# Reading the moving operand of 512-column products as two halves in turn

## The chip, the core and the metric

The kernel runs on one core of one Trainium2 chip. The metric is device time in microseconds (us) of one execution; the times given are medians over runs. In the profile, PE is TensorE (the matrix engine), PEld its loading of the stationary operand, DVE is VectorE, ACT is ScalarE, POOL is GpSimd and SP the engine from whose queue most transfers are issued. A TensorE product takes a stationary operand of 128 x 128, which is loaded first, and streams a moving operand of up to 512 columns past it; the result is added into a PSUM bank of 512 float columns per partition, of which there are eight.

## The reference

One layer of an encoder on 512 tokens with 1024 features. The mixer has two branches, bidirectional retention and a spatial gating unit (SGU), both fed by one input projection of 7168 columns; then comes a gated feed-forward part with a convolution of width 3:

```python
h = _rmsnorm(x, g_pre_mix)
q, k, v, g, u, sv, a_ret, a_sgu = jnp.split(h @ w_in, ...)
y_ret = _retention_branch(q, k, v, g, ret_decay_logit, w_ret_o)
y_sgu = _sgu_branch(u, sv, sgu_ln_g, sgu_ln_b, w_spatial, b_spatial, w_sgu_o)
merged = jax.nn.sigmoid(a_ret) * y_ret + jax.nn.sigmoid(a_sgu) * y_sgu
x = x + _rmsnorm(merged @ w_out, g_post_mix)
h2 = _rmsnorm(x, g_pre_ffn)
x = x + _rmsnorm(_conv_gated_mlp(h2, w_up, conv_w, conv_b, w_down), g_post_ffn)
```

All inputs and the output are float32. Nearly all the work is in the products with w_in, w_ret_o, w_sgu_o, w_out, w_up and w_down.

## The kernel before

Every float32 product is made of three faster ones. A helper `split` (L100) writes a value's high part (float32 rounded to the type fp32r, by ScalarE) and its low part (the difference, by VectorE); `mm3` (L230) then issues high x high, high x low and low x high into the same bank. So each product of the algorithm is three TensorE instructions, at L231, L232 and L233, or at L543 to L545, L924 to L926 and so on where they are written out. The weights come in from HBM through SP's queue as blocks of 128 x 1024 (`w_block`, `w_form`, `w_down`, fetched some blocks ahead by `w_get`), and are split on ScalarE and VectorE at L95 and L102 before TensorE can use them.

The stages, in order, all on one core:

- q and k (L336 to L351): eight banks, each 128 output features x 512 tokens; stationary is the weight, moving is `xh`/`xl`, the scaled input with features on partitions and 512 tokens along the row. The first k step (L342) runs in parts, as its operands arrive. Eight evacuations follow (L428 to L433).
- v, sv and g (`t_group`, L533): here tokens are stationary and the weight is moving, 512 columns of it; between the parts come the retention products of 256 columns.
- u and the gates (`Pair`, L746): a scheme with seven products in place of eight, on operands of 256 columns: `forms` (sums and differences) and halves T0, T1 of `xh`/`xl` taken by `Pair.x` (L768).
- w_ret_o and w_sgu_o (`f_block`, L735, called by `gated_pair`): weight stationary, 512 tokens moving (`ogh`, `yh` and their low parts). L886 and L893 multiply their results by the gates, from PSUM.
- w_out (`Down`, L906): tokens stationary, 512 columns of the weight moving. After each tile of 128 tokens come the norms, and `turn` (L985) transposes the tile on TensorE and writes `h2h` (L994, ScalarE) and `h2l` (L997, VectorE), features on partitions, 128 tokens at a time.
- w_up: `early` (L1017) makes the first four blocks in two halves of 256 tokens while the last tiles of w_out are still finished; then blocks of 512 tokens by `f_block`, and from block 4 to 19 couples, in which a `Pair` on `h2h`/`h2l` and their forms is mixed with two calls of `f_block` (48 products of 512 columns and 84 of 256 in a couple). `tile_done` makes the convolution and the gate from the banks.
- w_down (`products`, `add_whole`): products of 256 columns, then the last norm.

What sets the order: the instructions of each engine run in the order in which they were scheduled when the program was built, and each waits on semaphores for its operands. The tiles are aligned by hand: `slot` (L142) and the pads of `hi192`/`lo64` place weights at 0, 64 or 192 bytes against the row of the moving operand.

On the host, `_pairs` and `_rows` arrange the weights into blocks; the arrangement is not part of the device time.

## Time and profile before

| | us |
|---|---|
| time, median of 3 runs (818.19 to 819.24) | 818.48 |
| span of the profiled execution | 817.4 |
| TensorE, a product in flight | 809.1 |
| VectorE busy | 659.9 |
| ScalarE busy | 441.3 |
| GpSimd busy | 86.0 |

The page has no time of the profiled execution other than its span, from its first instruction to its last. A group's line gives the source line, engine, operation, output and inputs, the shape (stationary rows * columns, then moving and output size), the count, the busy time and the mean length of one. For a TensorE product that length runs from its entry into the array until its modelled end, so that lengths of neighbours overlap. A line of the timeline gives start, length and instruction. A line of a stretch gives the stretch, its length, then busy time and count for PE, PEld, DVE, ACT and POOL, then the granted TensorE clock, the share of the DMA engines and their rate.

### The profile page before, as it was taken

To read this page: it belongs to the slowest core of one execution; us is meant where nothing else is said; L and a number is where in the kernel's file an instruction comes from. 1 tells how busy PE (TensorE), PEld (TensorE's weight loads), DVE (VectorE), ACT (ScalarE), POOL (GpSimd) and SP (SyncE) were. 2 spreads that over 40 slices of the span, in tenths; PEclk is the share of its full clock that TensorE was granted. 3 is DMA by queue.
4 is the path that set the end of the run, shared out by engine and by line. 5 is a ranking of instruction groups with operands and counts; after the bars stand their busy time and mean duration, and the time that the engine had idled before them with its cause. 6 is when DMAs were issued, how large, how long until landed. Compare 5 with 4: busy or idle time off the path is not lost. (4 is left out here: it accounts for less than half of the span.)

```text
span 817.4 us, 13292 instructions
## 1 busy us (share of the span) xinstructions
PE 809.1 (99%) x5163; PEld 730.4 (89%) x5163; DVE 659.9 (81%) x1115; ACT 441.3 (54%) x777; POOL 86.0 (11%) x93
## 2 busy tenths in 40 slices
PE   9999999999999999999999999999999999999996
PEld 7888888888999999999988898899999898999996
DVE  7479897877898777767765659989999989987877
ACT  6546445536675444444445577556666666544441
POOL 0010000110001111132210210110111200000001
PEclk9999999999999999999999999999999999999998
DMA  8733222221333332233349111333333341233244
GB/s 287 259 117 103 78 79 77 77 79 65 103 103 105 104 103 90 91 103 103 107 165 335 53 51 66 104 103 104 104 103 103 103 156 52 77 130 110 97 155 155
DMA packets 29647, 93.24 MB, mean 114 GB/s; under 512 B 3536, under 2 KB 4432, under 8 KB 29584
## 3 DMA queue, kind: packets, MB, share of 16 engines
q1 hardware_dynamic: 27360, 86.76, 31.5%
q0 software_dynamic: 1360, 4.46, 1.6%
q10 hardware_dynamic: 864, 1.18, 0.4%
q8 instruction: 40, 0.66, 0.3%
q14 instruction: 23, 0.19, 0.1%
HBM read 88.19 MB, written 4.19 MB: 113 GB/s over the span
## 5 line engine op out<-in xcount | busy, mean ns | idle before, releaser
L102 DVE TENSOR_TENSOR wl<-raw,wh 128x1024 fp32r<-128x1024 f32 (+1 forms) x92 | 108.5, 1187 | 42.5 <-PE ps L762 20.0
L95 ACT ACTIVATE wf<-raw 128x512 fp32r<-128x512 f32 x140 | 85.0, 626 | 99.3 <-PE ps L232 34.0
L102 DVE TENSOR_TENSOR wf<-raw,wf 128x512 fp32r<-128x512 f32 x140 | 106.5, 773 | 25.3 <-ACT wf L95 24.5
L762 PE MATMUL ps<-sh,wf 128*128 128x256 f32 x640 | 118.8, 277 | 0.2 <-ACT c L95 0.2
L95 ACT ACTIVATE wh<-raw 128x1024 fp32r<-128x1024 f32 (+2 forms) x96 | 93.3, 983 | 39.2 <-PE ps L545 15.8
L762 PEld LDWEIGHTS ps<-sh,wf 128*128 128x128 f32 x640 | 100.9, 188 | 1.0 <-ACT c L95 0.4
L232 PE MATMUL ps<-h2l,wh 128*128 128x512 f32 (+1 forms) x256 | 92.5, 363 | 0.0
L231 PE MATMUL ps<-h2h,wh 128*128 128x512 f32 (+1 forms) x256 | 92.4, 364 | 0.0
L233 PE MATMUL ps<-h2h,wl 128*128 128x512 f32 (+1 forms) x256 | 92.3, 361 | 0.0
L762 PE MATMUL ps<-sl,wf 128*128 128x256 f32 x320 | 88.5, 277 | 0.0
L543 PE MATMUL ps<-wh,xh 128*128 128x512 f32 x192 | 75.0, 391 | 0.0
L544 PE MATMUL ps<-wl,xh 128*128 128x512 f32 x192 | 74.8, 390 | 0.0
L545 PE MATMUL ps<-wh,xl 128*128 128x512 f32 x192 | 74.7, 389 | 0.0
L762 PEld LDWEIGHTS ps<-sl,wf 128*128 128x128 f32 x320 | 60.1, 188 | 0.6
L1170 PE MATMUL ps<-dl,fh 128*128 128x256 f32 x216 | 59.8, 277 | 0.0
L1170 PE MATMUL ps<-dh,fh 128*128 128x256 f32 x216 | 59.7, 277 | 0.0
L1170 PE MATMUL ps<-dh,fl 128*128 128x256 f32 x216 | 59.7, 277 | 0.0
L233 PEld LDWEIGHTS ps<-h2h,wl 128*128 128x128 f32 x256 | 48.0, 188 | 7.7
L231 PEld LDWEIGHTS ps<-h2h,wh 128*128 128x128 f32 x256 | 47.8, 188 | 7.2 <-ACT h2h L994 0.3
L232 PEld LDWEIGHTS ps<-h2l,wh 128*128 128x128 f32 x256 | 48.1, 188 | 6.6
L762 PE MATMUL ps<-xh,wf 128*128 128x256 f32 x288 | 53.9, 278 | 0.0
L95 ACT ACTIVATE dh<-raw 128x768 fp32r<-128x768 f32 (+1 forms) x36 | 33.6, 949 | 34.4 <-DVE raw L204 18.9
(314 smaller groups left out, 2037.4 us busy)
## 6 DMA issues: line engine op xcount, KB each, us to landing
raw<-wall SPq DMA_DIRECT2D x144, 512.0 KB, 3.6
x<-x SPq DMA_DIRECT2D x24, 256.0 KB, 6.2
x<-x POOLq DMA_DIRECT2D x8, 256.0 KB, 2.4
xT<-xT SPq DMA_DIRECT2D x7, 256.0 KB, 4.7
xT<-xT POOLq DMA_DIRECT2D x4, 256.0 KB, 3.3
out<-zg SPq DMA_DIRECT2D x4, 256.0 KB, 2.0
raw<-wall SPq DMA_DIRECT2D x3, 256.0 KB, 4.7
out<-zs ACTq DMA_DIRECT2D x3, 256.0 KB, 2.4
```

What stands on the lines that cost most here:

```text
L95: return nc.scalar.activation(out=o, in_=i, func=AF.Copy)
L102: nc.vector.tensor_sub(lo, src, as32(hi))
L231: nc.tensor.matmul(o, ah, bh, start=start, stop=False, skip_group_check=skip)
L232: nc.tensor.matmul(o, ah, bl, start=False, stop=False, skip_group_check=skip)
L233: nc.tensor.matmul(o, al, bh, start=False, stop=stop, skip_group_check=skip)
L543: nc.tensor.matmul(acc[t], xh[k][:, c], wh[:, f], start=k == 0, stop=False)
L544: nc.tensor.matmul(acc[t], xh[k][:, c], wl[:, f], start=False, stop=False)
L545: part_end[0] = nc.tensor.matmul(acc[t], xl[k][:, c], wh[:, f], start=False, stop=k == KD - 1)
L762: self.last = nc.tensor.matmul(o, w_[:, c], a_, start=first and k == n == 0, stop=k == 3 and n == 2, skip_group_check=True,)
L1170: nc.tensor.matmul(o, a_[:, c], w_[:, f], start=j == t == i == 0, stop=j == DP - 1 and i == 2 and n not in (M2, M3, M4), skip_group_check= ...
```

## The change

Where a product streams 512 columns, the moving operand is read through a pattern `turns`: element 0 of the first half of the row, element 0 of the second half, element 1 of the first, and so on. The bank is still written in one run of 512 columns. Where the row holds its columns in natural order, the bank then holds them interleaved, and the evacuation puts them back with a read of step 2 (`in_turn`). Where it can be done, the row is stored even columns first instead, so that reading in turn gives the natural order: `h2h` and `h2l` by the writes in `turn`, the weights of v, sv, g and w_out by the host (`_turns`). With that, products of 256 columns of `h2h` and `h2l` read in turn as well; the shared forms, the products of 256 columns of `xh`, the retention and w_down keep their patterns. The two loads and the splits of the first input tile take 128 columns of each half.

```diff
...
 
     def copy(o, i):
         return nc.scalar.activation(out=o, in_=i, func=AF.Copy)
+
+    def two(t):
+        return t.rearrange("p (n c) -> p n c", n=2)
+
+    def turns(t, f=slice(0, 256)):
+        return t.rearrange("p (n c) -> p c n", n=2)[:, f, :]
+
+    def in_turn(o):
+        return o.rearrange("p (c n) -> p n c", n=2)
 
     def as32(t):
         return t.bitcast(F32)
...
     raw01 = [raw_tile() for _ in range(2)]
     x01 = [tmp("xT") for _ in range(2)]
     T0, T1 = slice(0, 256), slice(256, 512)
+    X0, X1 = slice(0, P), slice(P, 256)
     PIECES = slice(0, P), slice(P, S), slice(S, 2 * S)
     HALVES = slice(0, S), slice(S, 2 * S)
     for wp in PIECES[:2]:
         nc.scalar.dma_start(raw01[0][:, wp], wall[0, :, wp])
-    nc.sync.dma_start(x01[0][:, T0], xT[0, :, T0])
+    nc.sync.dma_start(two(x01[0])[:, :, X0], two(xT[0])[:, :, X0])
     nc.sync.dma_start(part[:, : PRE + KD], par[:, : PRE + KD])
-    nc.sync.dma_start(x01[0][:, T1], xT[0, :, T1])
+    nc.sync.dma_start(two(x01[0])[:, :, X1], two(xT[0])[:, :, X1])
     nc.sync.dma_start(raw01[0][:, PIECES[2]], wall[0, :, PIECES[2]])
     nc.sync.dma_start(x01[1], xT[1])
     for f in HALVES:
...
 
     xh, xl, xg = [], [], {}
 
-    def x_high(k, t, f):
-        return nc.scalar.activation(out=xh[k][:, f], in_=t[:, f], func=AF.Copy, scale=col(PRE + k))
+    def x_high(k, t, f=slice(0, 256)):
+        return nc.scalar.activation(out=two(xh[k])[:, :, f], in_=two(t)[:, :, f], func=AF.Copy, scale=col(PRE + k))
 
     def load_x(k):
         xh.append(blk(F32R, "xh"))
...
         t = tmp("xT")
         nc.sync.dma_start(t, xT[k])
         with behind():
-            x_high(k, t, slice(0, S))
+            x_high(k, t)
         return t
 
-    def x_low(k, t, f=slice(0, S)):
+    def x_low(k, t, f=slice(0, 256)):
         return nc.vector.scalar_tensor_tensor(
-            out=xl[k][:, f], in0=t[:, f], scalar=col(PRE + k), in1=as32(xh[k][:, f]), op0=ALU.mult, op1=ALU.subtract
+            out=two(xl[k])[:, :, f], in0=two(t)[:, :, f], scalar=col(PRE + k), in1=as32(two(xh[k])[:, :, f]),
+            op0=ALU.mult, op1=ALU.subtract,
         )
 
     lasts = []
...
 
         a, b, c = PIECES
         steps = (
-            (x_high, 0, x01[0], T0), (w_high, a, nc.vector.tensor_copy), (w_high, b), (w_low, a), (w_low, b),
-            (x_low, 0, x01[0], T0), (x_high, 0, x01[0], T1), (x_low, 0, x01[0], T1), (w_high, c), (w_low, c),
+            (x_high, 0, x01[0], X0), (w_high, a, nc.vector.tensor_copy), (w_high, b), (w_low, a), (w_low, b),
+            (x_low, 0, x01[0], X0), (x_high, 0, x01[0], X1), (x_low, 0, x01[0], X1), (w_high, c), (w_low, c),
         ) if i == 0 else (
-            (x_high, 1, x01[1], slice(0, S)), (x_low, 1, x01[1]),
+            (x_high, 1, x01[1]), (x_low, 1, x01[1]),
             (w_high, HALVES[0]), (w_low, HALVES[0]), (w_high, HALVES[1]), (w_low, HALVES[1]),
         )
         for f, *args in steps:
...
         wh, wl = w_get(1 if k < 4 else LOOK)
         if k == 0:
             for half in range(2):
-                for f in (T0, T1) if half == 0 else (slice(0, S),):
+                for f in (X0, X1) if half == 0 else (slice(0, 256),):
                     for a, b in ((wh, xh), (wl, xh), (wh, xl)):
                         for m in range(4 * half, 4 * half + 4):
                             nc.tensor.matmul(
-                                qk[m][:, f], a[:, m * P : (m + 1) * P], b[0][:, f],
+                                qk[m][:, 2 * f.start : 2 * f.stop], a[:, m * P : (m + 1) * P], turns(b[0], f),
                                 start=a is wh and b is xh and f.start == 0, stop=False, skip_group_check=True,
                             )
             continue
...
             x_scaled(k - 2, xts[k - 2])
         for m in range(8):
             c = slice(m * P, (m + 1) * P)
-            mm3(qk[m], wh[:, c], wl[:, c], xh[k], xl[k], False, k == KD - 1, True)
+            mm3(qk[m], wh[:, c], wl[:, c], turns(xh[k]), turns(xl[k]), False, k == KD - 1, True)
 
 
 
...
     for m in range(8):
         t = blk(n="qkraw")
         if m % 2:
-            nc.vector.tensor_copy(t, qk[m])
+            nc.vector.tensor_copy(two(t), in_turn(qk[m]))
         else:
-            copy(t, qk[m])
+            copy(two(t), in_turn(qk[m]))
         raw.append(t)
 
 
...
                 for kk in range(2):
                     k = 2 * kp + kk
                     f = slice(kk * S, (kk + 1) * S)
-                    nc.tensor.matmul(acc[t], xh[k][:, c], wh[:, f], start=k == 0, stop=False)
-                    nc.tensor.matmul(acc[t], xh[k][:, c], wl[:, f], start=False, stop=False)
-                    part_end[0] = nc.tensor.matmul(acc[t], xl[k][:, c], wh[:, f], start=False, stop=k == KD - 1)
+                    nc.tensor.matmul(acc[t], xh[k][:, c], turns(wh[:, f]), start=k == 0, stop=False)
+                    nc.tensor.matmul(acc[t], xh[k][:, c], turns(wl[:, f]), start=False, stop=False)
+                    part_end[0] = nc.tensor.matmul(acc[t], xl[k][:, c], turns(wh[:, f]), start=False, stop=k == KD - 1)
             yield acc
 
     vh, vl = {}, {}
...
             if between and k == n // 2:
                 between()
             c = slice(k * P, (k + 1) * P)
-            mm3(o, wh[:, c], wl[:, c], ah[k], al[k], k == 0, k == n - 1)
+            mm3(o, wh[:, c], wl[:, c], turns(ah[k]), turns(al[k]), k == 0, k == n - 1)
         return o
 
     class Pair:
...
             return o
 
         def x(self, first, t):
-            return lambda k: (self.h[first + k][:, t], self.l[first + k][:, t])
+            if self.h is xh:
+                return lambda k: (self.h[first + k][:, t], self.l[first + k][:, t])
+            f = slice(t.start // 2, t.stop // 2)
+            return lambda k: (turns(self.h[first + k], f), turns(self.l[first + k], f))
 
         def s(self, n):
             return lambda k: self.forms[n][k]
...
     for j in range(KD // 2):
         for o, t in gated_pair(ogh, ogl, late if j == 0 else None):
             b = (lo64("r", F32) if j == 0 else hi192("r", F32) if j < 3 else blk(n="r"))
-            v.tensor_mul(b, o, t)
+            v.tensor_mul(two(b), in_turn(o), two(t))
             r.append(b)
         mix(2 * j)
         mix(2 * j + 1)
     mh, ml = [], []
     for j in range(KD // 2):
         for i, (o, t) in enumerate(gated_pair(yh, yl)):
-            v.tensor_mul(t, o, t)
+            v.tensor_mul(two(t), in_turn(o), two(t))
             nc.gpsimd.tensor_tensor(out=t, in0=t, in1=r[2 * j + i], op=ALU.add)
             h_, l_ = blk(F32R, "mh"), blk(F32R, "ml")
             split(h_, l_, t)
...
             c = slice(t * P, (t + 1) * P)
             ah, al = self.a[0][k][:, c], self.a[1][k][:, c]
             o = self.acc[t][n]
-            nc.tensor.matmul(o, ah, bh, start=k == 0, stop=False)
-            nc.tensor.matmul(o, ah, bl, start=False, stop=False)
-            nc.tensor.matmul(o, al, bh, start=False, stop=k == self.nk - 1)
+            nc.tensor.matmul(o, ah, turns(bh), start=k == 0, stop=False)
+            nc.tensor.matmul(o, ah, turns(bl), start=False, stop=False)
+            nc.tensor.matmul(o, al, turns(bh), start=False, stop=k == self.nk - 1)
 
         def finish(self, t, n):
             for i, (wh, wl) in enumerate(self.held):
...
 
     h2 = []
 
+    def both(t):
+        return t.rearrange("p (c n) -> p c n", n=2)
+
     def turn(t, zs):
-        c = slice(t * P, (t + 1) * P)
+        c = slice(t * 64, (t + 1) * 64)
         pf = []
         for n in range(2):
             p = ps()
...
                 nc.tensor.transpose(pf[-1], zs[n][:, f * P : (f + 1) * P], ident)
             for k in range(4 * n, 4 * n + 4):
                 last = nc.scalar.activation(
-                    out=h2h[k][:, c], in_=pf[k], func=AF.Copy, scale=col(FFNG + k)
+                    out=turns(h2h[k], c), in_=both(pf[k]), func=AF.Copy, scale=col(FFNG + k)
                 )
                 v.scalar_tensor_tensor(
-                    out=h2l[k][:, c], in0=pf[k], scalar=col(FFNG + k), in1=as32(h2h[k][:, c]),
+                    out=turns(h2l[k], c), in0=both(pf[k]), scalar=col(FFNG + k), in1=as32(turns(h2h[k], c)),
                     op0=ALU.mult, op1=ALU.subtract,
                 )
         if t != 2:
...
             early_w.append(w_get(1))
             early_o.append(ps())
         wh, wl = early_w[e]
-        f = slice(q * 256, (q + 1) * 256)
+        f, half = slice(q * 256, (q + 1) * 256), slice(q * P, (q + 1) * P)
         for k in range(KD):
             c = slice(k * P, (k + 1) * P)
-            mm3(early_o[e][:, f], wh[:, c], wl[:, c], h2h[k][:, f], h2l[k][:, f], k == 0, k == KD - 1)
+            mm3(early_o[e][:, f], wh[:, c], wl[:, c], turns(h2h[k], half), turns(h2l[k], half), k == 0, k == KD - 1)
 
     dn_ = Down(mh, ml, KD, RES_OUT)
     zs = {}
...
     return a.reshape(a.shape[0] // P, P, a.shape[1])
 
 
+def _turns(a):
+
+    return a.reshape(*a.shape[:-1], 256, 2).swapaxes(-1, -2)
+
+
 def _pairs(a):
 
-    return a.reshape(4, 2, P, S).transpose(0, 2, 1, 3).reshape(4, P, 2 * S)
+    return _turns(a.reshape(4, 2, P, S).transpose(0, 2, 1, 3)).reshape(4, P, 2 * S)
 
 
 def _inter(a, b):
...
         _two(u).reshape(8, P, 1024),
         _gates(ar, i["w_ret_o"]),
         _gates(asg, i["w_sgu_o"]),
-        _rows(i["w_out"]),
+        _turns(_rows(i["w_out"]).reshape(KD, P, 2, S)).reshape(KD, P, D),
         _up(_inter(_parts(up[:, :DFF], NF, P), _parts(up[:, DFF:], NF, P))),
         _down(i["w_down"]),
     ])
```

## The prediction

> **What bounds the kernel now.** I read the head of the page first, then the products by line and shape, then stretches of TensorE's timeline, and last the busy time of the engines by stage.
>
> ```profile
> span 817.4 us, 13292 instructions
> PE 809.1 (99%) x5163; PEld 730.4 (89%) x5163; DVE 659.9 (81%) x1115; ACT 441.3 (54%) x777; POOL 86.0 (11%) x93
> PEclk9999999999999999999999999999999999999998
> ```
>
> TensorE has a product in flight for 99% of the span at the full granted clock, so a change of pace of its products goes into the time one for one, except where another engine is close behind. The three timed runs have a median of 818.48 us, 1.1 us over the profiled span; I make the sum against the span and add that 1.1 at the end as unchanged.
>
> The mean of one product in the groups (391 ns) is its length from entry to drain, and products overlap; the pace is the distance from start to start, which the timeline shows:
>
> ```profile
> 11.34 0.39 PE L231 MATMUL ps<-xh,wh 128*128 128x512 f32 x1
> ...
> 15.88 0.39 PE L233 MATMUL ps<-xh,wl 128*128 128x512 f32 x1
> ```
>
> From 11.34 to 15.88 us stand 20 products with no gap: 4.54 / 20 = 227 ns. Products of 256 columns:
>
> ```profile
> 101.80 0.28 PE L232 MATMUL ps<-q,k 128*128 128x256 f32 x1
> ...
> 102.93 0.28 PE L233 MATMUL ps<-q,k 128*128 128x256 f32 x1
> ```
>
> Ten in 1.13 us, 113 ns each. So time goes with the columns, 0.443 ns each, with no fixed part to be seen. That the array itself needs this long is doubtful, because of the first microseconds:
>
> ```profile
> 0.76 3.79 PE L324 MATMUL ps<-const-bfloat16-1.0 128*128 128x256 bf16 x17 [0.76 <-PEq L1455]
> 5.88 0.63 PE L342 MATMUL ps<-xh,wl 128*128 128x256 f32 x2
> L324 PE MATMUL ps<-const-bfloat16-1.0 128*128 128x256 bf16 x17 | 3.8, 418 | 0.8 <-PEq L1455 0.8
> 8.12 0.40 PE L342 MATMUL ps<-xl,wh 128*128 128x256 f32 x2
> L342 PE MATMUL ps<-xh,wl x12: 283/389/415, 5.9 to 10.2; 128*128 128x256 f32 x8, 128*128 128x512 f32 x4
> 5.60:6.50 0.90, 0.90 (x6) 0.90 (x5) 0.80 (x3) 0.20 (x1) 0.00 (x0) 1.00 1.04 364
> ```
>
> Sixteen steps of the bf16 warm-up take 3.79 less one length of 0.418, so 0.211 us each; the float products at 5.9 us take 0.63 - 0.415 = 0.215 us, so while the array is slow the element type makes no difference. A little later the same 256 columns take 0.40 - 0.28 = 0.12 us, and in the steady stages 0.113. (The granted clock in the window at 5.6 us says 1.00, so this slow pace is not a throttle that the page shows.) If the array goes from half to full pace between the two, some 213.3 ns, which lies between those, would become 106.7; the rows show 113.3, that is 17/16 of it; 512 columns at full pace would be 213.3, and 17/16 of that is 226.7, as measured. Estimated so, 6.7 ns in each 256 columns and 13.3 in each 512 are a shortfall of the stream, one lost step in sixteen. That it is 120 in one place and 113 in another, with the same shape and element type, says that the delivery of operands has a part in the pace. A lost step in 16 four-byte elements looks like a boundary every 64 bytes of the moving operand; that is inference, since each moving operand of before is one contiguous run and none is read in another pattern.
>
> [...]
>
> **The change part by part.** The order of the instructions on every engine and their number stay the same; only access patterns differ, so no wait is added and nothing moves past anything. First the products concerned:
>
> ```profile
> L543 PE MATMUL ps<-wh,xh 128*128 128x512 f32 x192 | 75.0, 391 | 0.0
> L232 PE MATMUL ps<-h2l,wh 128*128 128x512 f32 x192 | 75.0, 391 | 0.0
> L924 PE MATMUL ps<-wh,mh 128*128 128x512 f32 x64 | 25.1, 392 | 0.0
> L232 PE MATMUL ps<-gl,wh 128*128 128x512 f32 x64 | 25.0, 391 | 0.0
> L232 PE MATMUL ps<-yl,wh 128*128 128x512 f32 x64 | 25.0, 391 | 0.0
> L231 PE MATMUL ps<-xh,wh 128*128 128x512 f32 x56 | 21.8, 389 | 0.0
> L762 PE MATMUL ps<-h2h,wf 128*128 128x256 f32 x192 | 35.5, 277 | 0.0
> L762 PE MATMUL ps<-h2l,wf 128*128 128x256 f32 x96 | 26.6, 277 | 0.0
> L233 PE MATMUL ps<-h2h,wl 128*128 128x256 f32 x64 | 17.6, 279 | 0.0
> ```
>
> Each line with 512 columns has two sisters (high by high, high by low, low by high), so 3 x (192 + 192 + 64 + 64 + 64 + 56) = 1896, and 12 at L342: 1908. Products of 256 columns that also come to read in turns, since h2h and h2l are now stored with even tokens before odd ones: 192 + 96 + 3 x 64 = 480. The other products of 256 columns keep their pattern.
>
> 1. Pace. No row has a moving operand that alternates between two places 1 KB apart. Upper bound of the gain: the whole shortfall goes, 1908 x 13.3 = 25.4 us and 480 x 6.7 = 3.2 us. If both halves meet their 64-byte boundary at the same step, there is one boundary every 32 elements instead of 16, and half the shortfall would go: 12.7 and 1.6. On the other side, a loss: the rivals. I take 10 ns and 5 ns, between half and whole: 19.1 + 2.4 = 21.5 us.
>
> [...]
>
> 2. What VectorE hands back. In most stages it has slack, but here not:
>
> ```profile
> 275.00:297.30 22.30, 22.30 (x151) 20.36 (x150) 16.31 (x29) 9.45 (x16) 3.07 (x2) 1.00 0.29 95
> 536.30:556.80 20.50, 20.50 (x133) 18.56 (x132) 16.69 (x26) 11.88 (x21) 2.94 (x2) 1.00 0.34 115
> 556.80:618.30 61.50, 61.50 (x397) 55.69 (x396) 59.33 (x95) 38.19 (x68) 8.82 (x6) 1.00 0.29 97
> 618.30:659.80 41.50, 41.33 (x266) 37.24 (x265) 38.65 (x59) 25.66 (x44) 5.89 (x4) 1.00 0.34 113
> 677.50:702.00 24.50, 24.50 (x110) 20.31 (x109) 24.50 (x44) 14.77 (x23) 0.00 (x0) 1.00 0.19 65
> ```
>
> The third number is the busy time of TensorE, the fifth that of VectorE. From 556.8 to 702 us VectorE is busy 59.3 of 61.5, 38.7 of 41.5 and at the end all of 24.5 us: it splits the weights that TensorE needs next. TensorE's saving there is 6 couples x 48 + 96 = 384 products x 10 ns + 6 x 36 x 5 ns = 4.9 us, and cannot all be had. Bounds 0 to 4.9 us handed back; I take half, 2.5, since the couple before (16.7 of 20.5 us) lets it run a little ahead.
>
> 3. Evacuations read the bank with step 2 (8 of the first projection, 8 multiplies at L886, 8 at L893), and h2h, h2l are written alternately into two halves.
>
> ```profile
> L886 DVE TENSOR_TENSOR r<-ps,sig 128x512 f32<-128x512 f32 x8 | 5.4, 688 | 2.0 <-PE ps L233 1.3 <-ACT sig L808 0.8
> L798 DVE TENSOR_TENSOR c<-ps,c 128x256 f32<-128x256 f32 x8 | 3.3, 416 | 0.0
> L994 ACT ACTIVATE h2h<-ps,part x32: 347/367/401, 456.6 to 485.0; 128x128 fp32r<-128x128 f32 x32
> 482.61 3.15 DVE L997 SCALAR_TENSOR_TENSOR h2l<-ps,part,h2h 128x128 fp32r<-128x128 f32 x8 [1.08 <-ACT h2h L994]
> ```
>
> From 256 to 512 columns VectorE's multiply grows by 272 ns, 1.06 ns an element. If alternating places cost every element twice, a multiply of L886 or L893 takes 0.5 us more, under the 6 us that VectorE is idle in a stage of 22.3 (275 to 297 us): hidden; without that cover, 16 x 0.5 = 8 us. The eight steps of 128 columns for the last token tile (482.6 to 485.8 us) are not hidden, because the early products wait for each: 8 x 128 x 1.06 = 1.1 us on VectorE, and as much again if ScalarE's in front do not overlap. Bounds 0 and 2.2; I take 0.5, since the patterns have the same number of elements.
>
> 4. The start. The two loads of the first tile have runs of 512 bytes instead of 1 KB.
>
> ```profile
> 4.66 1.43 PE L342 MATMUL ps<-xh,wh 128*128 128x256 f32 x4
> xT<-xT SPq DMA_DIRECT2D x2, 128.0 KB, 2.9
> ```
>
> The first product waits on them at 4.66 us. As twice as many pieces they can cost little of the 2.9 us to landing; bounds 0 and 0.5, I take 0.1. The permuting of weights on the host changes no transfer.
>
> Sum: 21.5 - 2.5 - 0.5 - 0.1 = 18.4; 817.4 - 18.4 = 799.0, with 1.1 around it 800.1 us. With half the shortfall and the dearest bounds: 12.7 + 1.6 - 2.2 - 0.5 less half of the stretch's 3.3 = 10, 808.5 us; with all of it and nothing handed back 28.6, 789.9. The forecast's own range is 790 to 810.
>
> **The rivals.** A: the pace stays (the shortfall is the array's, or follows every 16 elements whatever their places). For it: it is the same in each stage, under DMA shares from 0.19 to 1.04; against it, the 120 ns above and the equal times at the slow pace. Time 818.5 plus items 3 and 4: 818 to 821.
>
> B: each run has its own boundary and a change of place adds one, so one step in eight is lost, 240 ns at 512 and 120 at 256. For it: 0.12 us was seen at 8.12 us. Against: it was seen with contiguous reads. Cost 1908 x 13.3 + 480 x 6.7 = 28.6 us: 847, up to 850 with item 3. It decides as soon as two alternating runs do not share their boundary.
>
> C: reading pairs. If the stream gets two neighbouring elements in one access, and an alternating pattern gets one, each product falls to the slow pace of the first microseconds: 426.7 ns at 512 and 213.3 at 256. Cost 1908 x 200 + 480 x 100 = 430 us: 1248 us. For it: at full pace four-byte columns fall short and at half pace they do not, so access is near its limit already. Against: nothing in the trace shows that neighbours share an access.
>
> [...]
>
> D: the change works, but VectorE keeps all 4.9 us of item 2: 802.5. This lies in the forecast's own range.
>
> **How the numbers follow.** Forecast with D 0.63, A 0.05, B 0.13, C 0.19. I lean to the forecast because the shortfall is real, stands on the delivery side, and repeats with 64 bytes of one run; I cannot exclude C, whose place in the trace is the same. 800 is the likeliest's time. The range takes in the forecast's own 790 to 810, A and B, and leaves out C: 790 to 850. About 0.2% (1.6 us) is what a measurement of this kernel can tell from no change: faster 0.63, same 0.05, slower 0.32.
>
> **What would show it.** The step from start to start of the 512-column products between 11 and 49 us: 213 to 220 ns right, 227 A, 240 B, about 427 C; the unchanged 256-column products (the shared forms) must stay at 113. The stretch of 145 us that begins at 556.8 would shorten by less than its products and show TensorE waiting for VectorE's weight splits; if it shows none, item 2 was too dear. The eight h2h and h2l steps of the last tile longer than 3.15 us would show item 3. The forecast is wrong if the step is 226 or more.

## The result and the profile after

The changed kernel takes 808.46 us (median of four runs, 805.31 to 809.66) where the kernel before takes 818.48 (818.19 to 819.24): a ratio of 0.987, 95% interval 0.9847 to 0.9893. It is faster, by 10.0 us instead of the 18.4 of the sum. The execution profiled took 809.66 us, with a span of 807.9.

The head of its page, and the first and last of the 168 products of 512 columns between the start and the wait at 47 us (columns: start in us, length, engine, line, operation):

```profile
span 807.9 us, 13298 instructions
PE 791.6 (98%) x5163; PEld 735.3 (91%) x5163; DVE 664.9 (82%) x1115; ACT 443.3 (55%) x777; POOL 84.8 (11%) x93
...
10.89 0.38 PE L240 MATMUL ps<-xh,wh 128*128 128x512 f32 x1
...
46.93 0.38 PE L242 MATMUL ps<-xh,wl 128*128 128x512 f32 x1
```

The step is (46.93 - 10.89) / 167 = 215.8 ns, where it was 227: the pace came, and in full. But TensorE, in flight for 99% of the span before, is so for 98% of a shorter one: 807.9 - 791.6 = 16.3 us without a product against 817.4 - 809.1 = 8.3. The view of TensorE's waits says for what, beside a wait of 0.8 us ahead of its first instruction in both. Before (us in total, times, longest):

```profile
PE ps L762 <- ACT c L95: 0.2, 1, 0.2
```

and after:

```profile
PE ps L449 <- ACT qkraw L95: 2.9, 1, 2.9
PE ps L773 <- ACT c L95: 2.7, 3, 1.0
PE ps L241 <- DVE h2l L1014: 1.8, 2, 1.0
PE ps L353 <- ACT xh L274: 0.8, 1, 0.8
```

The second is that of L762 grown (L773 is the same line of the changed kernel); the other three are new, the last of them at the start. To see where all of the time went, I paired the 5163 TensorE instructions of the two traces in order, and summed by how much the distance from each start to the next had changed. Distances over 245 ns for 512 columns, 126 for 256 and 120 for 128 count as gaps, by place. The sum is the difference of the spans, -9.5 us:

| what | forecast, us | measured, us |
|---|---|---|
| 512 columns in turns (1895 paired without a gap), 227.6 to 215.9 ns | -19.1 | -22.25 |
| 256 columns of h2 in turns (460), 114.7 to 111.6 ns | -2.4 | -1.43 |
| waits in the couples between 585 and 636 us | +2.5 | +2.43 |
| waits for h2h, h2l at 457-467 and 475-480 us | +0.5 | +2.32 and +0.89 |
| start, up to the first k of 512 columns | +0.1 | -0.18 |
| wait at L449 and half pace behind it, 47-55 us | none | +4.70 |
| 256 columns still contiguous (2574), 113.9 to 115.1 ns | none | +3.02 |
| waits ahead of the couples' stretch, 511-524 us | none | +0.98 |
| rest | | 0.0 |

So the products in turns give 23.7 us, and the waits and the slower contiguous products take 14 back. The largest of these was in no term of the sum. TensorE's rows there, and two windows of the busy time (columns: TensorE, weight loads, VectorE, ScalarE, GpSimd, granted clock, DMA share, GB/s):

```profile
50.23 1.13 PE L449 MATMUL ps<-ident,rstd 128*128 128x128 f32 x8 [2.91 <-ACT qkraw L95]
...
51.82 0.63 PE L556 MATMUL ps<-wh,xl 128*128 128x512 f32 x1
...
54.81 0.47 PE L554 MATMUL ps<-wh,xh 128*128 128x512 f32 x1
...
47.00:52.00 5.00, 2.09 (x13) 1.68 (x12) 4.50 (x8) 4.34 (x8) 0.41 (x1) 0.96 0.09 22
52.00:55.00 3.00, 3.00 (x9) 2.34 (x8) 2.97 (x6) 1.18 (x3) 0.00 (x0) 0.50 0.55 194
```

TensorE is idle for 2.9 us, and 1.6 us after it starts again come seven products at 427 ns ((54.81 - 51.82) / 7) instead of 216, where the clock is granted at 0.50. Idle time and slow products together are the 4.7 us.

L449 writes into a bank that the first of ScalarE's copies out of the q and k banks (`qkraw`) must have emptied. ScalarE's rows show when that was, with TensorE's first product behind it (L438 is L449 before). Before:

```profile
33.17 0.63 ACT L391 ACTIVATE x<-x 128x512 f32<-128x512 f32 x1 [3.02 <-DMA x<-x]
...
46.89 0.58 ACT L95 ACTIVATE qkraw<-ps 128x512 f32<-128x512 f32 x1
...
49.42 1.05 PE L438 MATMUL ps<-ident,rstd 128*128 128x128 f32 x8
```

After:

```profile
35.58 0.63 ACT L402 ACTIVATE x<-x 128x512 f32<-128x512 f32 x1 [3.39 <-DMA x<-x]
...
38.41 0.63 ACT L402 ACTIVATE x<-x 128x512 f32<-128x512 f32 x1 [1.17 <-DMA x<-x]
...
49.50 0.58 ACT L95 ACTIVATE qkraw<-ps 128x512 f32<-128x512 f32 x1
```

Before, the first copy ended at 47.47 us, 1.95 us ahead of TensorE. After, two things meet. TensorE is through with the first projection at 47.15 us, 2.3 us sooner, which uses up that lead. And ScalarE starts its copies at 49.50, 2.6 us later, since its waits for the loads of x end at 35.58 and 38.41, where before they ended at 33.17 and 35.76. The lead of 1.95 us and waits for x could both be read in the trace of before.

The products of 256 columns that kept their pattern did not keep their pace. A run of them at 102 us, where the prediction's rows had ten steps in 1.13 us:

```profile
102.49 0.28 PE L241 MATMUL ps<-q,k 128*128 128x256 f32 x1
...
103.68 0.28 PE L242 MATMUL ps<-q,k 128*128 128x256 f32 x1
```

Ten steps in 1.19 us, 119 ns against 113. By the pairing, the 946 contiguous products of the last projection, where nothing is read in turn, are as fast as before (113.8 ns in both); all 3.0 us lie on the others, which have products in turns around them (113.9 to 115.8 ns). Last, the evacuations and the writes of h2h and h2l (ns: least, median, most):

```profile
L900 DVE TENSOR_TENSOR r<-ps,sig x8: 681/688/692, 269.8 to 336.0; 128x512 f32<-128x512 f32 x8
L1011 ACT ACTIVATE h2h<-ps,part x32: 467/490/552, 449.3 to 479.0; 128x128 fp32r<-128x128 f32 x32
L1014 DVE SCALAR_TENSOR_TENSOR h2l<-ps,part,h2h x32: 420/444/455, 449.8 to 479.5; 128x128 fp32r<-128x128 f32 x32
476.02 3.92 DVE L1014 SCALAR_TENSOR_TENSOR h2l<-ps,part,h2h 128x128 fp32r<-128x128 f32 x8 [0.22 <-ACT h2h L1011]
461.88 0.35 PE L240 MATMUL ps<-h2h,wh 128*128 128x256 f32 x1
463.00 0.38 PE L241 MATMUL ps<-h2l,wh 128*128 128x256 f32 x1 [0.76 <-DVE h2l L1014]
```

L900 (L886 before) reads its bank with step 2 and takes 688 ns as before. L1011 and L1014 write alternately into two halves and take 490 ns (367 before) and 444 (350), and the early products wait for them. The eight steps of the last tile, in the fourth row, take 3.92 us instead of 3.15.

### The profile page after: what moved, and what is told of

It is laid out like the page before. It is cut to its first block, busy times and chain, and to the rows that moved or that the text cites. A ratio compares the mean times of both kernels' runs of the same rounds, so it can differ in the third digit from the quotient of the medians.

```text
span 807.9 us, 13298 instructions
## 1 busy us (share of the span) xinstructions
PE 791.6 (98%) x5163; PEld 735.3 (91%) x5163; DVE 664.9 (82%) x1115; ACT 443.3 (55%) x777; POOL 84.8 (11%) x93
## 5 line engine op out<-in xcount | busy, mean ns | idle before, releaser
L111 DVE TENSOR_TENSOR wl<-raw,wh 128x1024 fp32r<-128x1024 f32 (+1 forms) x92 | 109.6, 1200 | 34.0 <-PE ps L773 19.1
L111 DVE TENSOR_TENSOR wf<-raw,wf 128x512 fp32r<-128x512 f32 x140 | 108.7, 788 | 19.9 <-ACT wf L95 18.9
L773 PE MATMUL ps<-sh,wf 128*128 128x256 f32 x640 | 120.9, 278 | 2.0 <-ACT c L95 2.0
L773 PEld LDWEIGHTS ps<-sh,wf 128*128 128x128 f32 x640 | 101.7, 188 | 3.1 <-ACT c L95 2.4
L241 PE MATMUL ps<-h2l,wh 128*128 128x512 f32 (+1 forms) x256 | 90.4, 355 | 1.8 <-DVE h2l L1014 1.8
L240 PE MATMUL ps<-h2h,wh 128*128 128x512 f32 (+1 forms) x256 | 90.3, 355 | 0.1
L242 PE MATMUL ps<-h2h,wl 128*128 128x512 f32 (+1 forms) x256 | 90.1, 353 | 0.0
L773 PE MATMUL ps<-sl,wf 128*128 128x256 f32 x320 | 89.0, 278 | 0.0
L773 PEld LDWEIGHTS ps<-sl,wf 128*128 128x128 f32 x320 | 60.1, 188 | 0.4
L773 PE MATMUL ps<-xh,wf 128*128 128x256 f32 x288 | 54.5, 279 | 0.0
```

The lines of the kernel that those rows point to most:

```text
L111: nc.vector.tensor_sub(lo, src, as32(hi))
L240: nc.tensor.matmul(o, ah, bh, start=start, stop=False, skip_group_check=skip)
L241: nc.tensor.matmul(o, ah, bl, start=False, stop=False, skip_group_check=skip)
L242: nc.tensor.matmul(o, al, bh, start=False, stop=stop, skip_group_check=skip)
L773: self.last = nc.tensor.matmul(o, w_[:, c], a_, start=first and k == n == 0, stop=k == 3 and n == 2, skip_group_check=True,)
```

## The experiments

**One run of reads instead of two.** Everything as in the changed kernel, but the products, all except the early ones of w_up, read contiguous columns (so they come out in another order):

```diff
     def turns(t, f=slice(0, 256)):
-        return t.rearrange("p (n c) -> p c n", n=2)[:, f, :]
+        return t[:, 2 * f.start : 2 * f.stop]
...
```

> As the changed kernel, but the products read each moving operand in one run again (the early products of w_up still in turn); evacuations, writes of h2h and h2l and all loads stay changed, so the columns of several results are permuted. If the whole gain is the pace of the products: 227 ns again, no wait of 3 us at 47 us, and the time of before plus the dearer writes, 818.5 to 822 us. If part of the gain came from elsewhere (loads, order), below 817.

Measured: 821.91 us (820.95 to 824.12), ratio to the kernel before 1.0046 (1.0029 to 1.0062). The pace in its trace and its waits:

```profile
13.69 0.39 PE L243 MATMUL ps<-xh,wh 128*128 128x512 f32 x1
...
16.64 0.39 PE L244 MATMUL ps<-xl,wh 128*128 128x512 f32 x1
```

```profile
PE ps L356 <- ACT xh L277: 1.9, 1, 1.9
PE ps L244 <- DVE h2l L1017: 1.0, 1, 1.0
...
PE ps L776 <- ACT c L95: 0.2, 1, 0.2
```

13 steps in 2.95 us are 227 ns: the whole gain is the order of the reads. Without it the costs of the change stand alone, 3.3 us over the kernel before on the same chip (818.58); the waits for h2l and a later start stay, those at L449 and in the couples (0.2 us, as before) are gone. So the last two are not costs of the new patterns; they appear because TensorE comes sooner. Paired with the trace of before, the contiguous products of 256 columns are back at 113.8 ns (-0.07 us in all, against +3.02): they are slower only where other products are read in turn. How, is not shown by this.

**TensorE alone, with one pattern after another.** A small kernel that computes nothing of the reference: groups of 24 products of 512 columns with one moving tile, each group with another view of it, for instance

```python
halves     = t.rearrange("p (n c) -> p c n", n=2)         # 1 KB apart, in turn
quarters   = t.rearrange("p (n c) -> p c n", n=4)
steptwo    = t.rearrange("p (c n) -> p n c", n=2)         # evens, then odds
nearhalves = t.rearrange("p (b n c) -> p b c n", n=2, c=16)  # 64 bytes apart, in turn
pairs      = t.rearrange("p (n c e) -> p c n e", n=2, e=2)   # two of each half in turn
lines      = t.rearrange("p (n c e) -> p c n e", n=2, e=16)
```

> TensorE alone: groups of 24 products of 512 columns (48 of 256), each with its own stationary slice, one group for each way of reading the moving operand; nothing of the reference is computed. Boundary theory (the stream loses one step in sixteen when it passes to the next 64 bytes of one run, and the other half's element hides that): one run 227 ns from start to start, two halves in turn 216, quarters and eighths in turn 216, pairs of elements in turn 216, halves 64 bytes apart in turn 216, runs of 16 elements in turn 227 or more, every second element in two runs (a boundary every 8 elements) 240. Rival, two open lines (the chip holds two places open, each further one costs): halves 216, but quarters, eighths and every fourth element near 427. Rival, distance (the two places must be far apart): halves 64 bytes apart 227. For the 256-column runs: if their pace hangs on what stood in front of them, the groups after a group in turn take 116 to 120 ns and those after a run 113 to 114; if only on the alignment of the two operands, each alignment has one pace wherever it stands.

Measured, TensorE's timeline by group:

```profile
17.30 5.34 PE L56 MATMUL halves<-mov,sta 128*128 128x512 f32 x24
22.47 6.96 PE L56 MATMUL quarters<-mov,sta 128*128 128x512 f32 x24
29.26 11.88 PE L56 MATMUL eighths<-mov,sta 128*128 128x512 f32 x24
40.94 11.03 PE L56 MATMUL steptwo<-mov,sta 128*128 128x512 f32 x24
51.79 11.25 PE L56 MATMUL stepfour<-mov,sta 128*128 128x512 f32 x24
62.86 5.36 PE L56 MATMUL nearhalves<-mov,sta 128*128 128x512 f32 x24
68.06 8.31 PE L56 MATMUL pairs<-mov,sta 128*128 128x512 f32 x24
76.20 5.93 PE L56 MATMUL lines<-mov,sta 128*128 128x512 f32 x24
81.97 5.63 PE L56 MATMUL runagain<-mov,sta 128*128 128x512 f32 x24
87.43 5.76 PE L56 MATMUL runoff<-mov,sta 128*128 128x512 f32 x24
```

From the start of a group to the start of the next, by 24: halves 215, four places in turn 283, eight 487, step two 452, step four 461, two places 64 bytes apart 217, two of each half in turn 339, sixteen in turn 240, contiguous 228. So it is not the turning as such: with two places and single elements it removes the shortfall (215 and 217 against 228), and with four or eight places, a step, pairs or runs of sixteen it costs 12 to 260 ns. All three accounts that I had set out fail: the boundary theory had 216 for four and eight places and for pairs, the rival of two open lines had near 427 for four, and the rival of distance 227 at 64 bytes. Contiguous products with the stationary operand moved by 64 and 192 bytes took 233 and 229 ns, and those in turns 215.8 in each position.

The groups of 256 columns gave 111.7 ns in turns and 120.0, 119.9, 117.8 and 114.0 contiguous. Neither expectation holds: the last stands right behind a group in turns and is the quickest, and it has the same alignment as the one with 117.8.

A second kernel of this kind went nearer, and set contiguous products of 256 columns among others (`near16x` is four places 64 bytes apart, `shortrun` contiguous products of 256 alone; `mixlong` and `mixlongrun` are pairs of a contiguous 256 and a 512, 24 of each, with the 512 in turns or contiguous).

> Groups of 24 products of 512 columns (48 where one of 256 is in it) with TensorE alone, each group with one pattern of the moving operand. Two runs in turn, element by element, where the distance of the two is 16, 32, 128 or 256 bytes. Theory (two places in turn are free of the lost step because neighbouring accesses never ask for the same 64 bytes in a row twice, whatever the distance): 32 to 256 bytes all give 215 to 218 ns, 16 bytes (both elements in one line of 64) 227 to 233. [...] Runs of 4 and of 8 elements in turn: 300 and 270 by the fall from 339 (runs of 2) to 240 (runs of 16); of 64 elements: 227 to 233. A contiguous product of 256 columns with a product of 512 in turns behind it, against one with a contiguous 512 behind it: if the neighbours in turns cost the contiguous ones (as 3.0 us of the whole kernel seem to say), the pair takes 4 to 5 ns more than 113 + 216; the rival, that it is VectorE's and ScalarE's own accesses, lets the pair be 329 or 336 (113 to 120 for the 256).

```profile
23.84 20.88 PE L57 MATMUL near<-mov,sta 128*128 128x512 f32 x96
44.56 6.61 PE L57 MATMUL near16x<-mov,sta 128*128 128x512 f32 x24
...
73.78 5.92 PE L57 MATMUL shortrun<-mov,sta 128*128 128x256 f32 x48
79.54 8.24 PE L57 MATMUL mixlong<-mov,sta 128*128 128x256 f32 x48
87.61 8.48 PE L57 MATMUL mixlongrun<-mov,sta 128*128 128x256 f32 x48
95.93 5.66 PE L57 MATMUL mixshort<-mov,sta 128*128 128x256 f32 x48
```

The first row is four groups, two places 16, 32, 128 and 256 bytes apart: (44.56 - 23.84) / 96 = 215.8 ns, and all 96 have the same length, 379 ns. I expected 227 to 233 at 16 bytes, which did not come. At that distance the products cross from one 64 bytes to the next as often as a contiguous one does (after 16 elements), and lose nothing: the boundary of 64 bytes is not the cause of the shortfall. Runs of 4, 8 and 64 elements in turn gave 250, 243 and 229 ns (17.33 us for all 72, from 51.01 to 68.34, so 240.7 on average), and four places 64 bytes apart (near16x) 269. A pair takes (87.61 - 79.54) / 24 = 336 ns with the 512 in turns and (95.93 - 87.61) / 24 = 347 with it contiguous. The contiguous 256s among themselves ran at (79.54 - 73.78) / 48 = 120.0, so these are 120 + 216 and 120 + 227, the paces that each kind has alone: the pair shows no cost of the neighbour, and is the 336 of the rival. Why contiguous 256s are at 113 in one place and 120 in another, and what puts more of them at the slower pace in the changed kernel, stays open.

**The copies qkraw ahead of the forms of x**, on ScalarE and VectorE:

```diff
+    raw = []
+    for m in range(8):
+        t = blk(n="qkraw")
...
-    raw = []
-    for m in range(8):
-        t = blk(n="qkraw")
...
```

> As the changed kernel, but the eight copies out of the q and k banks stand before the first two sets of sums and differences (x_forms), so that ScalarE and VectorE come to them sooner. If the wait of 3.07 us near 47 us and the slow products behind it are due to ScalarE's order: the wait and the half-pace products vanish, 4 to 5 us less than the changed kernel, about 804. Rival (the wait is for the sum of squares or for weights, whatever the order): same time, 808, with the wait in the same place.

Measured: 807.91 us (806.96 to 809.06), ratio 0.9867 (0.985 to 0.9883). In the profile L449 starts at 47.31 us without a wait, and the half pace is gone, 4.7 us. But the forms and what follows them come later now, and TensorE waits 22 us on:

```profile
73.99 0.48 PE L554 MATMUL ps<-wh,xh 128*128 128x512 f32 x1 [1.36 <-DVE vl L565]
```

Between 69 and 79 us it has 2.65 us more than the kernel before, and on the contiguous 256s 1.2 us more than the changed kernel: no clear gain against 808.46, whose runs it overlaps, and not the 804 of the theory.

**The changed kernel once more:**

> The changed kernel itself once more. Theory: the first 50 us are set by a supply (SP's queue, the loads of x and w, ScalarE's rounding) that begins up to 2 us earlier or later in each execution, and only where it is late does TensorE, now quicker than the supply, stand idle before its products at L449 and then run some of them at half pace. Then this execution shows the same pace of 216 ns and the same waits at 457-467 us (+2.3 against the kernel before) and 475-480 (+0.9), while the 4.7 us near 47-55 us come and go: median 804 to 809 us, spread over 2 us or more. Rival: the wait near 47 us belongs to the order of the instructions and is there in every execution: it stands in this profile with 4 to 5 us again, and the median is 808 to 809.

Measured: 807.28 us (805.68 to 808.99), ratio 0.9859 (0.984 to 0.9877). Its profile (span 805.6 us) has the same pace, 2.0 and 0.9 us at the waits for h2l, and no wait at L449. ScalarE's copies there:

```profile
47.04 2.04 ACT L95 ACTIVATE qkraw<-ps 128x512 f32<-128x512 f32 x4
```

2.5 us sooner than in the first profile: ScalarE left its first wait for x at 34.73 us instead of 35.58 and had no second one. At the same time TensorE came to L449 at 48.82 us instead of 47.15, since its first products ran at half pace for longer: 213 ns for 256 columns from 6.36 to 8.92 us, in the first profile from 5.01 to 5.86, and 112 a little later in both (the start has 1.4 us more than before). So the wait comes and goes, with the time at which x lands and with the first microseconds, and the runs spread over 3 to 4 us, where those of before spread over 1.1. The theory holds; the rival, that the wait is there in every execution, falls.

**h2h and h2l written as two runs, the bank read with step 2:**

```diff
-                    out=turns(h2h[k], c), in_=both(pf[k]), func=AF.Copy, scale=col(FFNG + k)
+                    out=two(h2h[k])[:, :, c], in_=both(pf[k]), func=AF.Copy, scale=col(FFNG + k)
...
```

with `both` as `"p (c n) -> p n c"`, and the same for h2l.

> As the changed kernel, but h2h and h2l are written as two runs of 64 with the bank read in step 2, in place of alternately into two halves; the same elements land in the same places. If alternating writes are what makes these steps dear (490 and 444 ns against 367 and 350 before): back to about 367 and 350 ns, the waits of 1 us near 462 and 464 us go, 2 to 3.2 us less, about 805.5. Rival (the bank's order, not the write's, costs it): lengths stay near 490 and 444, time 808.

Measured: 803.61 us (802.73 to 804.64), ratio 0.9819 (0.9804 to 0.9833). The two instructions:

```profile
L1011 ACT ACTIVATE h2h<-ps,part x32: 345/367/404, 446.1 to 473.6; 128x128 fp32r<-128x128 f32 x32
L1014 DVE SCALAR_TENSOR_TENSOR h2l<-ps,part,h2h x32: 337/350/352, 446.5 to 474.0; 128x128 fp32r<-128x128 f32 x32
```

367 and 350 ns, as before the change: a step of 2 in reading a bank costs these nothing, the alternate order costs 123 and 94 ns (on ScalarE that is the write alone; VectorE also read `h2h` in that order). The waits at 457-480 us fall from 3.2 to 0.7 us over before. The rest of the difference of the two profiles lies at the start: no wait at L449 (-4.7 us), and 1.8 us more up to the first k of 512 columns. A second time:

> The run named runs once more, beside the next. Theory: 803 to 806 us; the waits at 457-480 us are 0.3 to 0.6 us over the kernel before instead of 3.2; the 4.7 us near 47 us are there or not, as in the run again. If the median of 803.6 was luck of the start, 805 to 806.

804.11 us (803.79 to 805.62), ratio 0.9828 (0.9811 to 0.9844): the gain came again. The waits for h2l were 1.2 us over before in this profile, more than the 0.3 to 0.6 expected. Its start was as quick as in the first profile of the changed kernel, and TensorE came to L449 as soon, but ScalarE's copies began at 46.95 us: the wait there was 0.2 us. Neither profile has the 2.9 us, so how the 3 to 5 us under the changed kernel divide between the writes (2 to 2.5 us by the waits for h2l) and luck of the start is not shown.

**Both edits together:**

> The copies qkraw ahead of the forms of x (as in the run sooner), and h2h, h2l written as two runs of 64 with the bank read in step 2 (as in the run runs). Theory: the second takes 2.6 us off the waits at 457-480 us, the first takes the wait near 47 us away and gives most of it back as a wait of VectorE at 69-79 us: 802 to 804 us, no better than runs alone (803.6). Rival, the two add up: 803.6 less 3 to 4.7, so 799 to 800.6 us.

805.94 us (805.04 to 807.07), ratio 0.9843 (0.9828 to 0.9858). This is over the 802 to 804 expected. They don't add up, and it is rather slower than with the writes alone: in both profiles with the early copies TensorE loses some 3 us at 69-79 us (3.1 in this one), where the wait at L449 is there only in some executions.

**Less work for VectorE in the couples:**

```diff
-        v.scalar_tensor_tensor(
-            out=c[:, 0 : S - 1], in0=o[:, 1:S], scalar=col(CW + 3 * m + 2), in1=c[:, 0 : S - 1],
+        if m < 8:
+            v.scalar_tensor_tensor(
+                out=c[:, 0 : S - 1], in0=o[:, 1:S], scalar=col(CW + 3 * m + 2), in1=c[:, 0 : S - 1],
...
```

> The changed kernel without the third tap of the convolution in the channel tiles 8 and up (left out of the computation), which takes 36 x 0.74 = 27 us of work off VectorE between 560 and 700 us and leaves TensorE's own products as they are. Theory: the waits of TensorE in the couples (3.4 us more than before, over 511-636 us) are for VectorE, whose busy share there is 0.98: they fall by 2.5 to 3.4 us, 805 to 806 us against 808.5. Rival: they are for ScalarE (its activations stand in front of VectorE's) or for a bank that is read slower: they stay, 808 to 809 us.

Measured: 803.62 us (801.81 to 804.56), ratio 0.9811 (0.9797 to 0.9826), 3.7 us under the changed kernel on the same chip (807.28), rather more than the 2.5 to 3.4 expected. One window of the changed kernel's busy time, then this version's waits and the same window:

```profile
556.80:618.30 61.50, 60.48 (x398) 56.20 (x398) 60.38 (x95) 38.67 (x69) 8.78 (x6) 1.00 0.31 104
```

```profile
PE ps L241 <- DVE h2l L1014: 1.5, 2, 1.0
PE ps L773 <- ACT c L95: 0.8, 1, 0.8
...
556.80:618.30 61.50, 61.50 (x412) 57.58 (x411) 52.92 (x86) 40.00 (x70) 9.91 (x7) 1.00 0.33 103
```

With VectorE at 52.9 of 61.5 us instead of 60.4, TensorE has no gap there and does 412 products in the time of 398. The two waits for c at 615 and 636 us are gone. They are written down to ScalarE's copy c, but only VectorE's work was changed, so ScalarE was late behind VectorE. The third wait for c, ahead of the couples' stretch, stays, at 520 us; the taps were left out only behind it, and ScalarE had stood 1.36 us for a `raw` of GpSimd just before that copy, so its cause is not shown.

**The other products of 256 columns in turns too**, on top of the two-run writes. The shared forms and the halves of x are read in turns and their banks with step 2; the forms of h2 are stored permuted; the weights of the last projection are permuted on the host:

```diff
-            return lambda k: self.forms[n][k]
+            return lambda k: tuple(turns(t, X0) for t in self.forms[n][k])
...
-            split(h_, l_, s_)
+            w2 = lambda t: t.rearrange("p (h n c) -> p h n c", h=2, n=2)
+            split(w2(h_), w2(l_), s_.rearrange("p (h c n) -> p h n c", h=2, n=2))
...
-                        o, a_[:, c], w_[:, f], start=j == t == i == 0,
+                        o, a_[:, c], turns(w_[:, f], X0), start=j == t == i == 0,
```

> The run named runs, and on top of it the shared forms of x and h2 and the weights of the last projection are also read as two halves in turn, in products of 256 columns: 2300 of the 2565 products that were still contiguous. Their results stand in the bank in natural order where the stored operand is permuted (h2's forms, by the step 2 in which VectorE and ScalarE read their source; the last projection's weights, on the host), and are read from the bank with step 2 otherwise. Theory: each goes from 115.1 to 111.6 ns start to start, 2300 x 3.5 = 8.1 us, on stages where TensorE is the bound, less what VectorE hands back in the couples (up to 768 x 3.5 = 2.7 us): 796 to 799 us against 803.6 to 806, and the products of 256 columns at 111 to 112 ns. Rival: reading SBUF with step 2 costs VectorE and ScalarE twice the time in the forms of h2 and the couples wait longer: 800 to 804. Second rival: in the middle of the kernel 256 columns have a fixed part that the turn doesn't touch (114 ns): no faster than runs.

Measured: 799.08 us (798.67 to 799.48), ratio 0.976 (0.9746 to 0.9775), 5.0 us under the two-run writes on the same chip (804.11). Two products of the last stage, and the wait in the couples:

```profile
689.75 0.28 PE L1194 MATMUL ps<-dh,fl 128*128 128x256 f32 x1
...
691.99 0.28 PE L1194 MATMUL ps<-dl,fh 128*128 128x256 f32 x1
...
PE ps L773 <- ACT c L95: 4.9, 4, 1.3
```

20 steps in 2.24 us, 112 ns. The time is at the upper end of the 796 to 799 expected. In the pairing the products of 256 columns that were contiguous in the changed kernel, most of them now in turns, go to 112.2 ns, 7.4 us less than there; the waits for c rise to 4.9 us, and 1.6 us of new waits come in the last projection. This version beats both kernels.

## Why the prediction was right, and where it was not

The main step, that the shortfall is on the side of the operands and that turning removes it, was right: 227 ns contiguous, 215.8 in turn. Its size in item 1 was too small for 512 columns: 11.7 ns of gain against 10 taken. The value between half and whole rested on the 64-byte boundary, and that inference falls with the pattern kernels. What stays is 215.8 ns, 2.5 over the 213.3 of a full-pace array, which was an estimate from the slow steps of 211 and 215 ns; no run shows 213.3 itself. For 256 columns 3.1 ns came where 5 were taken: 111.6 is 3.7 more than half of 215.8, where the prediction saw no fixed part.

Rivals A and B had 227 and 240 ns in the step between 11 and 49 us; 215.8 rules out both. Rival C, that an alternating pattern halves the pace, did not come; its 0.19 was my estimate. In the pattern kernels two places in turn lose nothing against contiguous (215 and 228 ns), four lose 55 ns (283), eight 260 (487), and step two is near C's 427 with 452. So a price of C's size came with step two and with eight places, and not with this pattern.

Item 2 was right in size, 2.43 us against 2.5 (D's 4.9 were too many), and in its engine, as the run with less work for VectorE shows. What would show it was named wrongly: no wait for weight splits, but waits for a bank that ScalarE has not copied, ScalarE being late behind VectorE. Another 0.98 us of waits came before the stretch that the item bounded; their cause is open.

Item 3 was right for the evacuations (688 ns both times) and mis-sized for the writes: 3.2 us against 0.5, over its upper bound of 2.2. The step that failed is "the patterns have the same number of elements", and that it priced only the eight steps of the last token tile. The steps became 123 and 94 ns longer, near the 136 of a doubling that the item named as its dear end, and the larger part of the waits, 2.3 us, stands at the second tile (463 and 466 us), whose steps the first early products wait for.

Item 4 was 0.1 and is -0.2 or, in the second profile of the changed kernel, +1.4: not a cost of the loads that can be told from how long the first products run at half pace (213 ns for 256 columns).

The steps that failed outright were "no wait is added" and the step before it, that a change of pace goes into the time one for one except where another engine is close behind. Only VectorE was looked for there. Near 49 us ScalarE was 1.95 us ahead. With 168 products x 11.8 ns = 2.0 us and the start TensorE comes 2.3 us sooner, and by these figures it would for that alone wait some 0.3 us; the second execution of the two-run writes, with ScalarE's copies as early as before, has 0.2 us. The rest of the 2.9 us is the late load of x, which comes and goes, and the half pace followed the idle time. And "the other products of 256 columns keep their pattern" was taken as keeping their pace: +3.0 us. Without these two, the forecast's terms as measured give -22.25 - 1.43 + 3.41 + 3.21 - 0.18 = -17.2, near the 18.4.

The time itself was met with luck. The prediction had 808.5 us for half the shortfall with the dearest bounds, and 808.46 was measured; but nearly the whole shortfall came, and terms that the sum did not have took it back.

## What to carry to other kernels

Before a gain in pace is summed over a kernel, look in every stage for what TensorE will need next from another engine, and how long before TensorE's own start it was done (49.42 - 47.47 = 1.95 us here): that lead is all the stage can give before it waits, and a supply that comes later in some executions takes from it too. Where a copy must write in two places in turn or read so, let it read its PSUM bank with the step and write runs: that was free on both ScalarE and VectorE here (367 and 350 ns, as before the change), the other way cost 27 to 34% (490 and 444 ns). And a pattern that helps with two places can cost with four (215 and 283 ns here, against 228 contiguous): measure the very pattern, by itself.

## What the runs showed of the hardware

Not expected: a 4-byte operand of 512 columns, read from two places in turn, streams at 215 to 217 ns, at any distance tried from 16 bytes to 1 KB, against 227 to 233 contiguous, 240 with sixteen elements of each place in turn, 339 with two, 452 with step two, 283 with four places and 487 with eight. Why is open; of the accounts tried, boundaries of 64 bytes do not fit the 16-byte distance, and a penalty for each change of place does not fit halves (215). After 2.9 us without a product TensorE ran seven products at 427 ns with the granted clock at 0.50; after 1.4 us without one (the run with the early copies) no such stretch came in the trace. Contiguous products of 256 columns ran at 114 to 120 ns in one kernel, and in the changed kernel more slowly in the stages that also have products in turns (115.8 against 113.9 ns) and unchanged in the last projection, which has none (113.8).
